# A gated-delta scan whose two heads share each TensorE operand: k and q side by side, u with zeros between

## The chip, the cores and the metric

The kernel runs on one core of one Trainium2 chip. The metric is device time in microseconds of one execution, lower is better. Before the change it is 1455.97 us, the median of three runs (1453.89 to 1456.44).

## The reference, cut to what matters

One inference step of two layers over 1024 prompt frames and 64 sample frames of width 1024. The even layer (gated convolution and banded attention) is not touched. The odd layer is a gated DeltaNet with 8 heads of 128 x 128 state, run in chunks of 64 frames:

```python
def gdn_chunk(S, q, k, v, g, beta):
    ...
    u = sol[..., :HD_C] - jnp.einsum('bhlk,bhkv->bhlv', sol[..., HD_C:], S)
    qk = jnp.einsum('blhd,bmhd->bhlm', q, k) * decay
    o = jnp.einsum('blhk,bhkv->blhv', q * jnp.exp(gc)[..., None], S) + jnp.einsum('bhlm,bhmv->blhv', qk, u)
    g_last = gc[:, -1]
    k_dec = k * jnp.exp(g_last[:, None, :] - gc)[..., None]
    S_new = jnp.exp(g_last)[..., None, None] * S + jnp.einsum('blhk,bhlv->bhkv', k_dec, u)
    return S_new, o
```

`sol` holds the solutions of a unit triangular system per chunk; it does not depend on `S`. What does depend on `S` is the recurrence over the chunks: `u` from `S`, `S_new` from `u`, and the output `o` from both.

## The kernel before, in words

Everything is float32. Heads are taken in four pairs `p`; a head of a pair is `q` (0 or 1). There are 17 chunks `c` of a pair (16 of the prompt, one of the sample, which starts from a given state), in three batches `b` of 6, 6 and 5 chunks.

Two kinds of TensorE work are woven together. One is the long projections (`project`, tile `pjt`): float32r matmuls with 384 or 320 columns, three for each of eight blocks (hi x hi, lo x hi, hi x lo), so three `pjt` rows in a listing are one step of it. The other is the delta work on small tiles. A generator class `Order` writes out TensorE's order by hand: each piece of work yields a time in nanoseconds after which its next step may stand, a running estimate (`order.now`, raised by `mm` and `tr`) plays the clock, and the projections fill what lies between. The order on TensorE is therefore fixed in the built program; the other engines' orders are set by a scheduler when it is built.

The delta work of one pair and batch is: `prepare` (transposes of k and q, their norms, `kd` = k by rows times a decay, `kt` = k by rows, the products k by k and q by k that become `An` and `KQD`), `substitute` and `join` (the triangular inverse, built up in 32-wide pieces: matmuls that are named `XT,Cb`, `M,X`, `XT,An`, `M,X`), `solve` (three groups of matmuls `cst,vt`, `BD,kt`, `vr,BD`, whose results replace k and v in place), `scan` (the recurrence) and `finish` (norm of the output and a transpose of `o`). While one batch is scanned, the next is solved and the one after is prepared, so these share the engines.

A scan step before, for both heads of the pair:
- `ks`: k and q of each head, 64 columns each, times that head's state. Four matmuls with a 128 x 64 stationary operand.
- DVE makes `u` (tile `us`, L1140) from the first half of `ks` and the solved v; ACT scales the second half into `qs` (L1142).
- `su`: `kd` of each head times `u` of that head. Two matmuls, with 64 rows and 128 columns of the array, into two PSUM buffers. DVE makes the new state from them (L1154).
- the inner output `o`: `KQD` times `u`, two matmuls of 64 x 64. They do not stand behind `su` but at the head of the next step, just ahead of the next `ks` (`outputs(*last)`). DVE adds `qs` (L1109), ACT squares the sum (L1113).

Halves 0 to 63 and 64 to 127 of a tile's partitions are the two heads. PSUM buffers of the delta work: tag `tr` has two, shared by the transposes, `An`/`KQD`, the inverse, `solve` and `o`; `su` has two; `ks` has one.

Of the kernel before, what the change touches and what calls it, by code (L numbers as in the profile page):

```python
# [107 lines left out]
class Net:  # L108
# [624 lines left out]
    def odd(self):  # L733
# [72 lines left out]
        def new_kq(p):  # L806
            KQ[p] = k1.tile([P, 2, NCH, 2, 64], F32, name="kq", tag="kq", bufs=2)
# [4 lines left out]
        def conv_dst(p, i):  # L812
            q = i % 2
            if i < 2:
                return 8 + 2 * p + q, KQ[p][:, 0, :, q, :]
            if i < 4:
                return 2 * p + q, KQ[p][:, 1, :, q, :]
            return 16 + 2 * p + q, V[p][:, :, q, :]
# [23 lines left out]
        def gates(ba):  # L842
            for n in ("beta", "egc", "dec", "gc"):
                G[n] = comp(n)
            beta, egc, dec, gc = (G[n] for n in ("beta", "egc", "dec", "gc"))
            buf = G["buf"] = k1.tile([P, NCH * P], F32, name="dbuf", tag="vt", bufs=2)
            x, ab, gg = (buf[:, 68 * i:68 * i + 68].rearrange("p (a c) -> p a c", c=NCH) for i in range(3))
# [22 lines left out]
            for j, c0 in enumerate((C_U, C_BD, C_H, C_H + 1)):  # L870
                w = cst[:, c0:c0 + P] if j < 2 else cst[:, c0:c0 + 1].broadcast_to([P, P])
                self.mm(ps[:, 68 * j:68 * j + 68], w, gf)
            gcf = gc.rearrange("p a c -> p (a c)")
# [5 lines left out]
            act.activation(egl.rearrange("p q a c -> p (q a c)"), ps[:, 136:272], AF.Exp)  # L879
            yield 1500  # L880
# [30 lines left out]
        def zeroed():  # L911
            for name, w in (("Cb", 32), ("BD", P)):
                Z[name] = self.kp.tile([P, NBM, w], F32, name=name)
                pool.memset(Z[name], 0.0)

        def prepare(p, b):
# [16 lines left out]
            ss = self.kp.tile([P, 2, NBM], F32, name="ss", tag="ss", bufs=2)[:, :, :nb]  # L933
            rr = self.kp.tile([P, 2, NBM], F32, name="rr", tag="rr", bufs=3)[:, :, :nb]
            tmp = self.kp.tile([P, 2, NBM], F32, name="rt", tag="rt", bufs=2)[:, :, :nb]
            junk = self.kp.tile([P, P], F32, name="junk", tag="junk", bufs=1)
            for i0 in range(0, nb, 4):
                m = min(4, nb - i0)
                for a in range(2):
                    ps = pst("tr").rearrange("p (c j) -> p c j", j=P)  # L940
                    for i in range(m):
                        c = c0 + i0 + i
                        self.tr(ps[:, i, :], kq[:, a, c].rearrange("p q t -> p (q t)"))
                    for i in range(m):
                        act.activation(junk, ps[:, i, :], AF.Square, accum_out=ss[:, a, i0 + i:i0 + i + 1])  # L945
                    if a == 0:
                        act.copy(out=kt[:, i0:i0 + m, :], in_=ps[:, :m, :])
                        dve.tensor_tensor(kd[:, i0:i0 + m, :], ps[:, :m, :],
                                          dec[:, p, c0 + i0:c0 + i0 + m].unsqueeze(2).broadcast_to([P, m, P]), ALU.mult)
                    yield 2160  # L950
            dve.tensor_scalar(ss, ss, EPS, None, ALU.add)
# [7 lines left out]
            for i0 in range(0, nb, 4):  # L959
                m = min(4, nb - i0)  # L960
                ps = pst("tr").rearrange("p (c j) -> p c j", j=P)
                for i in range(m):
                    for q in range(2):
                        self.mm(ps[64 * q:64 * q + 64, i, :], kq[:, 0, c0 + i0 + i, q, :], kq[:, :, c0 + i0 + i, q, :], share=1.6)
# [102 lines left out]
        def solve(p, b):  # L1067
# [3 lines left out]
            for i0 in range(0, nb, 4):  # L1071
                m = min(4, nb - i0)
                vt = V[p][:, c0 + i0:c0 + i0 + m].rearrange("p c q t -> p c (q t)")
                k = KQ[p][:, 0, c0 + i0:c0 + i0 + m].rearrange("p c q t -> p c (q t)")
# [8 lines left out]
                act.copy(out=k, in_=ps[:, :m, :])  # L1083
# [9 lines left out]
        def scan(p, b):  # L1093
# [3 lines left out]
            egc, egl = G["egc"], G["egl"]  # L1097
            vt = V[p].rearrange("p c q t -> p c (q t)")
            S = state.get(p)

            def outputs(i, o4, so, u, qs):

                o = pst("tr")[:, 0:P]
                for q in range(2):
                    h = slice(64 * q, 64 * q + 64)
                    self.mm(o[h], KQD[h, i, :], u[h], share=1.6, tile_position=(64 * q, 64 * q))
                a = i % 4
                if qs is not None:
                    dve.tensor_tensor(o4[:, a, :], o, qs, ALU.add)  # L1109
                else:  # L1110
                    dve.tensor_copy(o4[:, a, :], o)
                junk = self.kp.tile([P, P], F32, name="junk", tag="junk", bufs=1)
                act.activation(junk, o4[:, a, :], AF.Square, accum_out=so[:, 0, a:a + 1])  # L1113
                if a == 3 or i == nb - 1:
                    order.add(f"fin{p}.{b}.{i - a}", 3, finish(p, b, i - a, a + 1, o4, so), [])

            last = None
            for i in range(nb):
                if i % 4 == 0:
# [5 lines left out]
                c = c0 + i  # L1125
# [5 lines left out]
                qs = None  # L1131
                if last:
                    outputs(*last)
                if S is not None:
                    ks = pst("ks")
                    for a in range(2):
                        for q in range(2):
                            self.mm(ks[64 * q:64 * q + 64, P * a:P * a + P], kq[:, a, c, q, :], S[:, q, :], share=1.6)
                    u = self.kp.tile([P, P], F32, name="us", tag="us", bufs=2)
                    dve.tensor_tensor(u, ks[:, 0:P], vt[:, c, :], ALU.add)  # L1140
                    qs = self.kp.tile([P, P], F32, name="qs", tag="qs", bufs=2)
                    act.activation(qs, ks[:, P:2 * P], AF.Copy, scale=egc[:, p, c:c + 1])  # L1142
                    yield 850
                else:
                    u = vt[:, c, :]
                su = []
                for q in range(2):
                    h = slice(64 * q, 64 * q + 64)
                    su.append(pst("su")[:, 0:P])
                    self.mm(su[q], kd[h, i, :], u[h])  # L1150
                Sn = self.kp.tile([P, 2, P], F32, name="S", tag="S", bufs=3)
                for q in range(2):
                    if S is not None:
                        dve.scalar_tensor_tensor(Sn[:, q, :], S[:, q, :], egl[:, q, p, c:c + 1], su[q], ALU.mult, ALU.add)  # L1154
                    else:
                        dve.tensor_copy(Sn[:, q, :], su[q])
                S = Sn
                last = i, o4, so, u, qs
                yield 1110
            outputs(*last)  # L1160
# [4 lines left out]
        def finish(p, b, i0, m, o4, so):  # L1165
# [16 lines left out]
            for q in range(2):  # L1182
                act.activation(ch(mo[:, q, :64 * m]), ps[:, :m, 64 * q:64 * q + 64], AF.Copy, scale=par[:, P_ON:P_ON + 1])
# [150 lines left out]
```

## Time and profile before

| what | value |
|---|---|
| runs | 1456.44, 1455.97, 1453.89 us |
| profiled execution, its own time | 1450.93 us |
| its span | 1449.1 us |
| TensorE busy (PE) | 1372.1 us, 95% |
| weight loads (PEld) | 1233.9 us, 85% |
| VectorE (DVE), ScalarE (ACT), GpSimd (POOL) | 877.6, 678.0, 312.9 us |
| first `ks` and last `su` | 796.0 and 1288.7 us |

Engines are named PE (TensorE), PEld (its weight loads), DVE, ACT, POOL and SP. A row of the timeline gives start, length, engine, line, operation, output<-inputs, the part of the array and the shape, and a count; in brackets stands the idle time ahead of it and what ended it. Plain float32 matmuls leave two records each, float32r matmuls and transposes one. A matmul's length there overlaps its neighbours', so times on PE are read below as the distance from one start to the next. L119 is the helper that issues every matmul and L124 the one that issues every transpose; the names of the tiles tell which is which.

### The profile page before, as it was taken

The numbers are of one execution on the slowest core, as the hardware profiler recorded it, in microseconds if no ns is written. First come the engines' busy times: TensorE is split into PE (matmuls) and PEld (weight loads), VectorE is DVE, ScalarE is ACT, GpSimd is POOL, SyncE is SP. The second block draws the span as 40 slices with busy tenths as digits, with TensorE's granted clock in tenths as the row PEclk, the third lists the DMA queues.
The fourth block names the chain that finished last, engine by engine and source line by source line (L and its number), as shares of the span: only waits on it lengthen the run. The fifth ranks groups of instructions, "written<-read, shape, count | busy, mean of one in ns | idle before, by whom it ended". The sixth has DMA issues, their size and how long they took to land. (4 is left out here: it accounts for less than half of the span.)

```text
span 1449.1 us, 28440 instructions
## 1 busy us (share of the span) xinstructions
PE 1372.1 (95%) x10600; PEld 1233.9 (85%) x10600; DVE 877.6 (61%) x2497; ACT 678.0 (47%) x1776; POOL 312.9 (22%) x810
## 2 busy tenths in 40 slices
PE   8999999999999999899878999999899989998996
PEld 6989998998999899888768778788887877888985
DVE  7675257137435754777887768676765756433654
ACT  7643345144334456675546444544453534323642
POOL 3000000000100014420345325140523152210322
PEclk9999999999999999999989999999999999999998
DMA  7402111210210274541523112122211232337454
GB/s 260 143 16 89 57 52 52 80 53 26 90 61 30 66 244 135 190 140 37 119 73 79 40 29 77 33 52 44 68 30 31 62 95 67 95 123 234 141 197 162
DMA packets 114378, 133.12 MB, mean 92 GB/s; under 512 B 35568, under 2 KB 81336, under 8 KB 114240
## 3 DMA queue, kind: packets, MB, share of 16 engines
q1 hardware_dynamic: 83280, 105.01, 24.8%
q10 hardware_dynamic: 30960, 26.31, 5.6%
q8 instruction: 83, 1.36, 0.4%
q14 instruction: 55, 0.45, 0.1%
HBM read 99.91 MB, written 34.51 MB: 93 GB/s over the span
## 5 line engine op out<-in xcount | busy, mean ns | idle before, releaser
L119 PE MATMUL pjt<-hhi,wlo 128*128 128x384 f32 (+1 forms) x1768 | 617.7, 349 | 1.5 <-DVE wlo L165 1.5
L119 PE MATMUL pjt<-hhi,whi 128*128 128x384 f32 (+1 forms) x1768 | 583.7, 330 | 5.8 <-ACT whi L164 2.4
L119 PE MATMUL pjt<-hlo,whi 128*128 128x384 f32 (+1 forms) x1768 | 576.1, 330 | 0.7 <-DVE hlo L391 0.6
L119 PEld LDWEIGHTS pjt<-hhi,wlo 128*128 128x128 f32 x1768 | 337.6, 191 | 25.6 <-issue 11.7
L119 PEld LDWEIGHTS pjt<-hhi,whi 128*128 128x128 f32 x1768 | 337.6, 191 | 12.4 <-ACT whi L164 3.7
L119 PEld LDWEIGHTS pjt<-hlo,whi 128*128 128x128 f32 x1768 | 335.6, 190 | 1.8 <-DVE hlo L391 1.8
L165 DVE TENSOR_TENSOR wlo<-wf,whi 128x512 fp32r<-128x512 f32 x222 | 154.3, 721 | 153.0 <-ACT whi L164 149.5
L164 ACT CAST whi<-wf 128x512 fp32r<-128x512 f32 x222 | 129.6, 618 | 165.0 <-PE pjt L119 123.4
L612 ACT ACTIVATE pr<-pr,mx 128x640 f32<-128x640 f32 (+5 forms) x72 | 50.9, 707 | 89.4 <-DVE mx L611 88.9
L784 DVE SCALAR_TENSOR_TENSOR kq<-pjt,par,kq 128x384 f32<-128x384 f32 (+2 forms) x144 | 71.6, 497 | 2.9
L348 POOL TENSOR_TENSOR sqa<-sqa,sq 128x384 f32<-128x384 f32 (+1 forms) x36 | 39.7, 1103 | 151.7 <-ACT sq L346 151.6
L573 POOL MEMSET bias<- 64x64 f32 x8 | 1.3, 163 | 321.0 <-DMA bias<-Gd 228.2
L609 DVE CUSTOM_DVE_ANT_0 pr<-sc,bias 128x640 f32<-128x640 f32 (+5 forms) x72 | 48.0, 666 | 26.7 <-PE sc L119 25.9
L991 POOL TENSOR_TENSOR px<-AL 48x14 f32<-48x14 f32 (+6 forms) x168 | 46.9, 279 | 61.5 <-DMA AL<-Sd 52.5
L1154 DVE SCALAR_TENSOR_TENSOR S<-S,egl,su 128x128 f32<-128x128 f32 x128 | 40.6, 343 | 29.3 <-PE su L119 28.9
L755 POOL TENSOR_TENSOR so<-so 128x4 f32<-128x4 f32 (+2 forms) x72 | 16.7, 232 | 175.4 <-DVE so L748 117.2
L945 ACT ACTIVATE junk<-tr 128x128 f32<-128x128 f32 x136 | 37.7, 277 | 33.9 <-PE tr L124 29.6
L992 POOL TENSOR_TENSOR AL<-AL,px 48x14 f32<-48x14 f32 (+6 forms) x168 | 46.8, 278 | 9.4
L119 PE MATMUL pjt<-mhi,whi 128*128 128x384 f32 x128 | 44.4, 347 | 3.7 <-ACT mhi L164 3.7
L124 PE MATMUL pt<-cst,pr 128*128 128x128 f32 (+1 forms) x280 | 43.4, 270 | 4.5 <-DVE pr L614 2.9
L1113 ACT ACTIVATE junk<-o 128x128 f32<-128x128 f32 x68 | 21.0, 309 | 51.4 <-DVE o L1109 42.2
L119 PE MATMUL pjt<-mlo,whi 128*128 128x384 f32 x128 | 44.5, 348 | 0.3 <-DVE mlo L165 0.2
(250 smaller groups left out, 2210.8 us busy)
## 6 DMA issues: line engine op xcount, KB each, us to landing
wf<-in_w_in SPq DMA_DIRECT2D x128, 256.0 KB, 3.5
wf<-in_w_out SPq DMA_DIRECT2D x96, 256.0 KB, 3.5
mf<-mixd SPq DMA_DIRECT2D x32, 192.0 KB, 3.4
x<-in_x SPq DMA_DIRECT2D x8, 384.0 KB, 6.2
xg<-in_x SPq DMA_DIRECT2D x2, 1536.0 KB
xd<-xg SPq DMA_DIRECT2D x2, 1536.0 KB
Dd<-dbuf ACTq DMA_DIRECT2D x16, 192.0 KB, 2.1
od<-o ACTq DMA_DIRECT2D x12, 256.0 KB, 2.5
```

The lines of the kernel that those rows point to most:

```text
L119: return self.pe.matmul(out, lhsT=lhsT, rhs=rhs, start=start, stop=stop, **k)
L124: return self.pe.transpose(out, in_, self.ident[0:k, 0:k])
L164: self.act.copy(out=hi, in_=x)
L165: (eng or self.dve).tensor_tensor(lo, x, hi.bitcast(F32), ALU.subtract)
L348: pool.tensor_tensor(acc, acc, sq, ALU.add)
L609: dve.tensor_tensor_reduce(out=cut(pr[0:nq, :nk]), in0=sc[0:nq, :nk // nw, :nw], in1=cut(b["bias"][a][0:nq, j0:j0 + nk]), scale=1.0, scala ...
L612: act.activation(pr[0:nq, :nk], pr[0:nq, :nk], AF.Exp, bias=mx[0:nq, 1:2], scale=1.0, accum_out=mx[0:nq, 2:3])
L784: dve.scalar_tensor_tensor(oi, ch(ps[:, i0 + j + 1:i0 + j + 1 + m]), cw[j], oi, ALU.mult, ALU.add)
L945: act.activation(junk, ps[:, i, :], AF.Square, accum_out=ss[:, a, i0 + i:i0 + i + 1])
L991: pool.tensor_tensor(t, AL[:, j + 1:16, j:j + 1].broadcast_to([lanes, m, w]), x.broadcast_to([lanes, m, w]), ALU.mult)
L992: pool.tensor_tensor(o, o, t, ALU.add)
L1154: dve.scalar_tensor_tensor(Sn[:, q, :], S[:, q, :], egl[:, q, p, c:c + 1], su[q], ALU.mult, ALU.add)
```

## The change

A pair's k and q now lie in one tile as four blocks of 64 for each chunk: k of head 0, q of head 0, q of head 1, k of head 1. So `ks` is one 128 x 128 stationary operand for each head, two matmuls in place of four, and the two heads' results lie in two columns of `ks`. `u` of both heads is one tile of 128 x 256 with zeros in the two blocks that belong to no head; two such tiles are zeroed once. `su` is one matmul of `kd` with 256 columns. DVE makes `u` and ACT scales q's part in two operations of 64 partitions each where there was one of 128; ACT writes straight into the output tile `o4`. The inner output is written directly behind `su`, and its two 64 x 64 matmuls go to the other half of the partitions (head 0 in the upper). In `prepare` the transposes are of k and q together, `kt` is copied in two halves, and `kd` is made from `kt`. The number of transposes and of the other matmuls is the same. The yields of a step are 1050 and 1110 where they were 850 and 1110.

```diff
 def new_kq(p):
-    KQ[p] = k1.tile([P, 2, NCH, 2, 64], F32, name="kq", tag="kq", bufs=2)
+    KQ[p] = k1.tile([P, NCH, 4, 64], F32, name="kq", tag="kq", bufs=2)
...
 def zeroed():
-    for name, w in (("Cb", 32), ("BD", P)):
+    for name, sh in (("Cb", [P, NBM, 32]), ("BD", [P, NBM, P]), ("u0", [P, 2, P]), ("u1", [P, 2, P])):
...
 def prepare(p, b):
...
-    for a in range(2):
+    for q in range(2):
         ps = pst("tr").rearrange("p (c j) -> p c j", j=P)
         for i in range(m):
-            c = c0 + i0 + i
-            self.tr(ps[:, i, :], kq[:, a, c].rearrange("p q t -> p (q t)"))
+            self.tr(ps[:, i, :], kq[:, c0 + i0 + i, 2 * q:2 * q + 2, :].rearrange("p a t -> p (a t)"))
...
-        if a == 0:
-            act.copy(out=kt[:, i0:i0 + m, :], in_=ps[:, :m, :])
-            dve.tensor_tensor(kd[:, i0:i0 + m, :], ps[:, :m, :], ...
+        h = slice(64 * q, 64 * q + 64)
+        act.copy(out=kt[h, i0:i0 + m, :], in_=ps[h, :m, :])
         yield 2160
+    dve.tensor_tensor(kd[:, i0:i0 + m, :], kt[:, i0:i0 + m, :], ...
...
 def scan(p, b):
...
-    if last:
-        outputs(*last)
+    u = Z[f"u{c % 2}"]
     if S is not None:
         ks = pst("ks")
-        for a in range(2):
-            for q in range(2):
-                self.mm(ks[64 * q:64 * q + 64, P * a:P * a + P], kq[:, a, c, q, :], S[:, q, :], share=1.6)
-        u = self.kp.tile([P, P], F32, name="us", tag="us", bufs=2)
-        dve.tensor_tensor(u, ks[:, 0:P], vt[:, c, :], ALU.add)
-        qs = self.kp.tile([P, P], F32, name="qs", tag="qs", bufs=2)
-        act.activation(qs, ks[:, P:2 * P], AF.Copy, scale=egc[:, p, c:c + 1])
-        yield 850
+        for q in range(2):
+            self.mm(ks[:, col[q]], kq[:, c, 2 * q:2 * q + 2, :].rearrange("p a t -> p (a t)"), S[:, q, :])
+        for q in range(2):
+            dve.tensor_tensor(u[half[q], q, :], ks[half[q], col[q]], vt[half[q], c, :], ALU.add)
+        for q in range(2):
+            o = half[1 - q]
+            act.activation(o4[o, a, :], ks[o, col[q]], AF.Copy, scale=egs[o, p, c:c + 1])
+        yield 1050
...
-    for q in range(2):
-        h = slice(64 * q, 64 * q + 64)
-        su.append(pst("su")[:, 0:P])
-        self.mm(su[q], kd[h, i, :], u[h])
+    su = pst("su")[:, 0:2 * P]
+    self.mm(su, kd[:, i, :], u.rearrange("p q j -> p (q j)"))
...
+    o = pst("tr")[:, 0:P]
+    for q in range(2):
+        self.mm(o[half[1 - q]], KQD[half[q], i, :], u[half[q], q, :], share=1.6, tile_position=(64 * q, 64 - 64 * q))
+    if S is not None:
+        dve.tensor_tensor(o4[:, a, :], o, o4[:, a, :], ALU.add)
...
     yield 1110
-    outputs(*last)
```

In the orders below `tr<-us,KQD` (before) and `tr<-u_7069,KQD` (after) are the inner output, `tr<-cst,vt`, `tr<-BD,kt` and `tr<-vr,BD` the three groups of `solve`, `tr<-kq` the products that become `An` and `KQD`. TensorE, first pair, where the scan of batch 0 meets the solve of batch 1; before:

```order
L119 MATMUL tr<-M,X 32x32 x12
L119 MATMUL pjt<-hhi_6899,wlo 128x320
L119 MATMUL pjt<-hhi_6899,whi 128x320
L119 MATMUL pjt<-hlo_6900,whi 128x320
L119 MATMUL tr<-us,KQD 64x128 x2
L119 MATMUL ks<-S,kq 64x128 x4
L124 MATMUL tr<-cst,vt 128x128 x4
L119 MATMUL tr<-BD,kt 128x128 x4
L119 MATMUL su<-us,kd 128x128 x2
L119 MATMUL tr<-kq 64x128 x8
L119 MATMUL tr<-vr,BD 128x128 x4
L119 MATMUL tr<-us,KQD 64x128 x2
```

and now:

```order
L119 MATMUL ks<-S,kq 128x128 x2
L119 MATMUL tr<-M,X 32x32 x12
L119 MATMUL tr<-kq 64x128 x8
L119 MATMUL su<-u_7069,kd 128x256
L119 MATMUL tr<-u_7069,KQD 64x128 x2
L124 MATMUL tr<-cst,vt 128x128 x4
L119 MATMUL tr<-BD,kt 128x128 x4
L119 MATMUL ks<-S,kq 128x128 x2
L119 MATMUL tr<-kq 64x128 x2
```

The products `tr<-kq` have moved ahead of `su`, and the output stands between `su` and the first group of `solve`, where `ks` stood. The same engine a little earlier, where the inverse of batch 1 begins; before:

```order
L119 MATMUL tr<-us,KQD 64x128 x2
L119 MATMUL ks<-S,kq 64x128 x4
L119 MATMUL tr<-XT,Cb 32x16 x24
L124 MATMUL tr<-cst,kq 128x128
L119 MATMUL pjt<-hhi_6477,wlo 128x384
```

and now:

```order
L119 MATMUL su<-u_7069,kd 128x256
L119 MATMUL tr<-u_7069,KQD 64x128 x2
L124 MATMUL tr<-cst,kq 128x128
L119 MATMUL tr<-XT,Cb 32x16 x24
L119 MATMUL pjt<-hhi_6477,wlo 128x384
```

A transpose of `prepare` has moved from behind the inverse's first group to ahead of it. On DVE, the rows that follow the two `BD` copies out of `tr` at the first of the two places; before:

```order
L1063 TENSOR_TENSOR BD<-tr,sT 32x6x32 x2
L784 SCALAR_TENSOR_TENSOR kq<-pjt,par,kq 128x6x64
L752 TENSOR_TENSOR rt<-rt,rr 128x2x5
L1109 TENSOR_TENSOR o_8324<-tr,qs 128x128
L784 SCALAR_TENSOR_TENSOR kq<-pjt,par,kq 128x6x64
```

and now:

```order
L1071 TENSOR_TENSOR BD<-tr,sT 32x6x32 x2
L784 SCALAR_TENSOR_TENSOR kq<-pjt,par,kq 128x6x64
L751 SCALAR_TENSOR_TENSOR rt<-rr,ss 128x2x5
L1145 SCALAR_TENSOR_TENSOR S<-S,egl,su 128x128 x2
L784 SCALAR_TENSOR_TENSOR kq<-pjt,par,kq 128x6x64
L752 TENSOR_TENSOR rt<-rt,rr 128x2x5
L1153 TENSOR_TENSOR o_8339<-tr,o_8339 128x128
```

The addition that empties the output's PSUM buffer now stands behind the two state updates of the same step.

More of the change, by code (lines that the diff above doesn't have):

```diff
@@ L814, in conv_dst @@
             if i < 2:
[L815 removed]
+                return 8 + 2 * p + q, KQ[p][:, :, 3 * q, :]
             if i < 4:
[L817 removed]
+                return 2 * p + q, KQ[p][:, :, 1 + q, :]
             return 16 + 2 * p + q, V[p][:, :, q, :]
@@ L842, in gates @@
         def gates(ba):
-            for n in ("beta", "egc", "dec", "gc"):
+            for n in ("beta", "egc", "egs", "dec"):
                 G[n] = comp(n)
-            beta, egc, dec, gc = (G[n] for n in ("beta", "egc", "dec", "gc"))
+            beta, egc, dec = (G[n] for n in ("beta", "egc", "dec"))
             buf = G["buf"] = k1.tile([P, NCH * P], F32, name="dbuf", tag="vt", bufs=2)
+            gc = G["gc"] = buf[:, 1600:1668].rearrange("p (a c) -> p a c", c=NCH)
             x, ab, gg = (buf[:, 68 * i:68 * i + 68].rearrange("p (a c) -> p a c", c=NCH) for i in range(3))
@@ L872, in gates @@
                 self.mm(ps[:, 68 * j:68 * j + 68], w, gf)
+            for q in range(2):
+                self.mm(ps[64 * q:64 * q + 64, 272:340], cst[:, C_U + 64 - 64 * q:C_U + 128 - 64 * q], gf)
             gcf = gc.rearrange("p a c -> p (a c)")
@@ L1082, in solve @@
                     self.mm(ps[:, i, :], kt[:, i0 + i, :], BD[:, i0 + i, :])
-                act.copy(out=k, in_=ps[:, :m, :])
+                act.copy(out=k, in_=ps[:, :m, :].rearrange("p c (q t) -> p c q t", q=2))
                 yield 900
@@ L1096, in scan @@
             kd, KQD = rr["kd"], rr["KQD"]
-            egc, egl = G["egc"], G["egl"]
+            egs, egl = G["egs"], G["egl"]
             vt = V[p].rearrange("p c q t -> p c (q t)")
+            half = [slice(0, 64), slice(64, P)]
+            col = [slice(0, P), slice(P, 2 * P)]
             S = state.get(p)
-            def outputs(i, o4, so, u, qs):
-                o = pst("tr")[:, 0:P]
-                for q in range(2):
-                    h = slice(64 * q, 64 * q + 64)
[L1106 to L1117, printed above, removed]
             for i in range(nb):
-                if i % 4 == 0:
+                c, a = c0 + i, i % 4
+                if a == 0:
                     if len(fins) > 2:
@@ L1153, in scan @@
                     if S is not None:
-                        dve.scalar_tensor_tensor(Sn[:, q, :], S[:, q, :], egl[:, q, p, c:c + 1], su[q], ALU.mult, ALU.add)
+                        dve.scalar_tensor_tensor(Sn[:, q, :], S[:, q, :], egl[:, q, p, c:c + 1], su[:, col[q]], ALU.mult, ALU.add)
                     else:
-                        dve.tensor_copy(Sn[:, q, :], su[q])
+                        dve.tensor_copy(Sn[:, q, :], su[:, col[q]])
+                o = pst("tr")[:, 0:P]
+                for q in range(2):
+                    self.mm(o[half[1 - q]], KQD[half[q], i, :], u[half[q], q, :], share=1.6, tile_position=(64 * q, 64 - 64 * q))
+                if S is not None:
+                    dve.tensor_tensor(o4[:, a, :], o, o4[:, a, :], ALU.add)
+                else:
+                    dve.tensor_copy(o4[:, a, :], o)
                 S = Sn
-                last = i, o4, so, u, qs
+                junk = self.kp.tile([P, P], F32, name="junk", tag="junk", bufs=1)
+                act.activation(junk, o4[:, a, :], AF.Square, accum_out=so[:, 0, a:a + 1])
+                if a == 3 or i == nb - 1:
+                    order.add(f"fin{p}.{b}.{i - a}", 3, finish(p, b, i - a, a + 1, o4, so), [])
                 yield 1110
-            outputs(*last)
             if b == NB - 1:
```

31 lines of the change are left out of this document (16 added, 15 removed).

## The prediction

> **What bounds the kernel now.** I read the page first, then the busy time of the stretch in which the scans run, then TensorE's timeline inside a few scan steps, last the waits.
>
> ```profile
> span 1449.1 us, 28440 instructions
> ...
> PE 1372.1 (95%) x10600; PEld 1233.9 (85%) x10600; DVE 877.6 (61%) x2497; ACT 678.0 (47%) x1776; POOL 312.9 (22%) x810
> ```
>
> ```profile
> 796.00:1291.00 495.00, 473.69 (x4764) 394.00 (x4762) 321.30 (x1183) 219.97 (x751) 153.67 (x592) 0.99 0.24 59
> ```
>
> In the second row the columns are the stretch, its length, then busy time of PE, PEld, DVE, ACT and POOL, the granted clock, the DMA share and GB/s. All scan steps lie in it. PE idles for 495.0 - 473.7 = 21.3 us of it, the clock is full, DVE is busy for 65%, ACT for 44%. So the stretch ends when PE has worked off its list: PE time taken out of a step comes off the span, unless it turns into waiting. Since busy time on PE counts overlapping and draining matmuls, what a step really costs is read from the starts.
>
> ```profile
> 1226.45 0.34 PE L119 MATMUL pjt<-hlo,whi 128*128 128x384 f32 x1
> 1226.72 0.44 PE L119 MATMUL tr<-us,KQD 64*64 64x128 f32 x4
> 1227.09 0.66 PE L119 MATMUL ks<-S,kq 128*64 128x128 f32 x8
> 1227.68 0.44 PE L119 MATMUL pjt<-hhi,wlo 128*128 128x384 f32 x1
> 1227.96 0.34 PE L119 MATMUL pjt<-hhi,whi 128*128 128x384 f32 x1
> 1228.13 0.34 PE L119 MATMUL pjt<-hlo,whi 128*128 128x384 f32 x1
> ...
> 1228.65 0.34 PE L119 MATMUL pjt<-hlo,whi 128*128 128x384 f32 x1
> 1228.92 0.49 PE L119 MATMUL su<-us,kd 64*128 64x128 f32 x4
> 1229.35 0.44 PE L119 MATMUL pjt<-hhi,wlo 128*128 128x384 f32 x1
> 1229.63 0.34 PE L119 MATMUL pjt<-hhi,whi 128*128 128x384 f32 x1
> ```
>
> Projection matmuls of 384 columns start 0.17 to 0.18 us apart (0.175 below). From the last one ahead of the output (1226.45) to the second behind `ks` (1227.96) are 1.51 us; two steady distances of 0.175 taken off, output and `ks` cost 1.16 us. From 1228.65 to 1229.63, `su` costs 0.98 - 0.35 = 0.63 us. A step costs PE 1.79 us. Part of it is no streaming: the distance into the output and into `su` is 0.27 instead of 0.175, and the first projection matmul behind a group holds the next off by 0.28.
>
> **The change, part by part.** What the new shapes cost is read from full-array float32 matmuls with projections on both sides, and from an output group that follows such matmuls directly:
>
> ```profile
> 791.85 0.34 PE L119 MATMUL pjt<-hlo,whi 128*128 128x384 f32 x1
> 792.03 0.61 PE L119 MATMUL tr<-vr,BD 128*128 128x128 f32 x4
> 792.39 0.42 PE L119 MATMUL pjt<-hhi,wlo 128*128 128x384 f32 x1
> 792.65 0.34 PE L119 MATMUL pjt<-hhi,whi 128*128 128x384 f32 x1
> ...
> 818.35 0.31 PE L119 MATMUL pjt<-hlo,whi 128*128 128x320 f32 x1
> 818.49 0.61 PE L119 MATMUL tr<-vr,BD 128*128 128x128 f32 x4
> 819.03 0.44 PE L119 MATMUL tr<-us,KQD 64*64 64x128 f32 x4
> 819.39 0.41 PE L119 MATMUL pjt<-hhi,wlo 128*128 128x320 f32 x1
> 819.64 0.31 PE L119 MATMUL pjt<-hhi,whi 128*128 128x320 f32 x1
> ```
>
> `ks`: two float32 matmuls of 128 x 128 (four records) are exactly the first group: 792.65 - 791.85 - 0.35 = 0.45 us. There is no extra distance into it (0.18).
> `su` and output: the new `su` is one matmul of 256 columns, which streams as many columns as the four records of 128, so I take it at the price of `tr<-vr,BD`; the second group then is the new pair `su`, output: 819.64 - 818.35 - 2 x 0.15 = 0.99 us (0.15 is the steady distance at 320 columns). The other half of the partitions for the output changes nothing that these rows show; I cost it at nothing.
> New step: 0.45 + 0.99 = 1.44 us, 0.35 less. How many steps, and what the other engines do in them:
>
> ```profile
> L119 PE MATMUL ks<-S,kq 128*64 128x128 f32 x512 | 42.1, 285 | 0.0
> ...
> L1140 DVE TENSOR_TENSOR us<-ks,vt x64: 251/292/294, 796.7 to 1287.4; 128x128 f32<-128x128 f32 x64
> L1142 ACT ACTIVATE qs<-ks,egc x64: 349/368/405, 797.6 to 1287.7; 128x128 f32<-128x128 f32 x64
> ```
>
> 64 steps have a state (8 records each): 64 x 0.35 = 22 us less PE time. The four first chunks without a state change by less than half a microsecond together.
>
> ```profile
> L164 ACT CAST whi<-wf 128x512 fp32r<-128x512 f32 x222 | 129.6, 618 | 165.0 <-PE pjt L119 123.4
> ...
> L508 ACT CAST ks<-ks 64x512 fp32r<-64x512 f32 x8 | 5.0, 619 | 0.2
> L947 ACT COPY kt<-tr 128x512 f32<-128x512 f32 x12 | 7.0, 580 | 0.0
> ```
>
> The two casts of 512 elements take the same on 64 and on 128 partitions, so I price each half of a split operation like the whole. DVE: one more addition per step at 0.29 us: 64 x 0.29 = 19 us, and eight copies of u for the first chunks. 321 + 21 of 495 us: 69%, still beside PE. ACT: one more scaling of 0.37 in each step, 24 us, and the second copies of `kt`, twelve at 0.58 and twelve shorter ones, at most 14 us: 220 + 38 = 258 us, 52%. What hides both is the projection matmuls. In the order, nine now usually stand between `ks` and `su` (1.6 us) where six stood (1.05); that covers the second addition. Where that cover is missing, `su` waits 0.29 us longer. `kd` read from `kt` and not from PSUM, two zeroed tiles, two small matmuls and one exponential in `gates`: under 1 us on PE; I take 1 us for the longer `prepare` at the first pair, where nothing is scanned yet.
>
> **What comes back as waiting.** The output takes one of the two `tr` buffers. It used to stand where `ks` (0.59 us) came behind it; now the next `tr` user is often directly behind. The built program says which buffer each gets. At the first place shown in the orders, `M,X`, the output, `cst,vt` and `BD,kt` all have the same one, one after the other: `cst,vt` can start only when DVE has done both state updates and the output's addition, `BD,kt` only when ACT has copied `vr`. This is so in all four pairs. At the second place `cst,kq` and `XT,Cb` share one in two pairs (in a third, output and `XT,Cb` with a single transpose between). With two more, there are 13 places at which a `tr` user stands at once behind its predecessor in the same buffer. Before there are five, plus four with one short group between. Their price, from the rows of before:
>
> ```profile
> 814.62 0.43 PE L119 MATMUL tr<-us,KQD 64*64 64x128 f32 x4 [0.68 <-ACT vt L1088]
> ...
> 816.48 0.68 PE L119 MATMUL tr<-BD,kt 128*128 128x128 f32 x4 [0.24 <-DVE KQD L967]
> 852.48 0.66 PE L124 MATMUL tr<-cst,o 128*128 128x128 f32 x4 [1.38 <-ACT M L1050]
> 862.50 0.49 PE L119 MATMUL tr<-BD,kt 128*128 128x128 f32 x2 [0.66 <-ACT vr L1079]
> 927.31 0.33 PE L124 MATMUL tr<-cst,kq 128*128 128x128 f32 x1 [0.79 <-ACT M L1050]
> ...
> 1082.33 0.44 PE L119 MATMUL tr<-us,KQD 64*64 64x128 f32 x4 [0.68 <-ACT vt L1088]
> ```
>
> Five waits of 0.66 to 1.38, mean 0.84, sum 4.2, and four of 0.24: 5 us, which go. 13 x 0.84 = 11 come, and about 1 for the outputs that wait for `M,X`: 12. Ends: nothing comes, if DVE and ACT happen to be ahead (-5 us net); 13 x 1.38 = 18, and nothing goes (+18). I take +7, from the mean, as the new places are of the same kind.
>
> **Sum.** -22 + 7 + 1, and +1 for `su` where its cover is short: -13 us. The profiled execution took 1450.9 us (span 1449.1 and 1.8 around it), 5.0 below the median of the runs, so 1438 for such an execution and 1443 for the median. Ends: -22 - 5 = -27 gives 1429, -22 + 18 + 2 = -2 gives 1454. Behind the last output 34 projection matmuls stand ahead of the last transpose of `finish`, 40 before: at most 1 us less cover, inside these ends.
>
> [...]
>
> **Rivals.**
> Full gain: the new `tr` places cost no more than the old ones. DVE idles for 31% of the stretch even then, and PE comes to these places no later than now. -20 to -27, about 1433. Against it: the four links in one buffer are a chain by construction.
> Gain eaten: the waits return 19 to 25 us, within 0.2% of before (3 us, about what a measurement of this kernel can tell from no change); 1456. For it: in the crowded places `An` and `KQD` come out of a chain on DVE, so PE arriving earlier only waits longer, and 22 us are no more than 5.6 per pair. Against: the crowded places hold five or six of a pair's 16 steps; the others have nine projection matmuls on each side.
> Slower, by one mechanism: DVE's addition of the output stands behind the two state updates and needs what ACT has written into `o4`. If ACT is late, DVE stands still, the next `u` is late, and `su` waits in every step. It decides from 0.35 us a step on; at 0.5 us, 64 x 0.5 - 22 = +10, about 1466. For it:
>
> ```profile
> PE su L119 <- DVE us L1140: 3.3, 2, 2.6
> ```
>
> Such waits exist, two of 64 now, 3.3 us. Against: ACT has from `ks` to the end of `su`, over 2 us, for two operations of 0.37.
> [...]
>
> **How the numbers follow.** Forecast (-4 to -19): 0.50; full gain 0.26; eaten 0.10; overlap lost 0.03; slower 0.11. Faster by over 0.2%: 0.76; within: 0.13; slower: 0.11. The range leaves out the slower case and the far end of the full gain: 1430 to 1457. The forecast's own range is 1437 to 1452.
>
> **What the profile of the changed kernel would show.** Right: `ks` in four records, 0.36 us from its start to the next projection, no 0.27 ahead of it; `su` in two records, 0.43 to 0.54 to the output; per pair some 3 us of waits of PE at `cst,vt` (ended by DVE's addition of the output) and `BD,kt` (by ACT's `vr`); the last `su` near 1275 instead of 1288.7. Wrong: `su` or the moved output longer than taken here; PE waiting for `u` in many steps; idle time in the stretch above 40 us.

## The result and the profile after

The changed kernel takes 1477.62 us, median of four runs (1475.43 to 1481.26), against 1456.2 beside it: ratio 1.0166, 95% interval 1.0135 to 1.0197. (The ratios here and in the table below come from the record; they are not exactly the quotients of the medians, which here would give 1.0147.) It is slower by 21 us where 13 us less were forecast. Its profiled execution took 1479.56 us, span 1477.8; the page of it:

```profile
span 1477.8 us, 27890 instructions
...
PE 1369.1 (93%) x10212; PEld 1251.3 (85%) x10212; DVE 897.8 (61%) x2581; ACT 714.4 (48%) x1865; POOL 310.1 (21%) x812
```

The same stretch as before (columns: stretch, length, busy time of PE, PEld, DVE, ACT, POOL, granted clock, DMA share, GB/s):

```profile
796.00:1291.00 495.00, 449.00 (x4253) 392.84 (x4252) 333.33 (x1237) 247.71 (x817) 150.14 (x584) 0.96 0.23 54
```

PE now idles for 46 us of it (21.3 before), and the clock has fallen from 0.99 to 0.96. The last `su` starts at 1316.0, not at 1288.7.

A step itself costs what was forecast, where it is read here. PE's timeline, first `su` and output, then `ks`:

```profile
1222.90 0.34 PE L119 MATMUL pjt<-hlo,whi 128*128 128x384 f32 x1
1223.08 0.59 PE L119 MATMUL su<-u,kd 128*128 128x256 f32 x2
1223.60 0.43 PE L119 MATMUL tr<-u,KQD 64*64 64x128 f32 x4
1223.96 0.44 PE L119 MATMUL pjt<-hhi,wlo 128*128 128x384 f32 x1
1224.24 0.34 PE L119 MATMUL pjt<-hhi,whi 128*128 128x384 f32 x1
...
1225.12 0.60 PE L124 MATMUL tr<-cst,kq 128*128 128x128 f32 x4
1225.55 0.61 PE L119 MATMUL ks<-S,kq 128*128 128x128 f32 x4
1225.92 0.42 PE L119 MATMUL pjt<-hhi,wlo 128*128 128x384 f32 x1
```

From 1222.90 to 1224.24 are 1.34 us; two steady distances of 0.175 off, `su` and output cost 0.99, as forecast. `ks` takes 0.37 to the next start.

What PE waits for between 780 and 1340 us (total, times, longest), after:

```profile
PE tr L124 <- DVE o L1176: 18.7, 5, 7.1
PE tr L124 <- DVE o L1153: 6.0, 5, 1.5
PE tr L119 <- ACT kt L953: 4.7, 7, 1.5
PE pjt L119 <- DVE pjt L778: 3.9, 2, 2.9
PE su L119 <- DVE u L1131: 2.9, 2, 1.8
PE tr L119 <- ACT vr L1087: 2.7, 4, 0.7
```

and the row of before that answers to the first of these (L1175 there is the same line):

```profile
PE tr L124 <- DVE o L1175: 4.4, 2, 3.1
```

The second and the last rows of after are the forecast chain in one `tr` buffer. The first is not: it is `finish`, whose transposes of `o` wait for DVE's scaling by the norm. And `su <- u`, the mechanism of the slower rival, is 2.9 us, less than the 3.3 of before.

**The long wait followed back.** Of the 18.7 us the longest three are 5.07 us (at 877.34), 4.13 (1031.77) and 7.14 (1194.76). The first of them, from after's timelines of PE, DVE, POOL and ACT:

```profile
871.89 0.38 PE L119 MATMUL tr<-vr,BD 128*128 128x128 f32 x2
877.34 0.66 PE L124 MATMUL tr<-cst,o 128*128 128x128 f32 x2 [5.07 <-DVE o L1176]
```

```profile
858.78 0.28 DVE L1153 TENSOR_TENSOR o<-tr,o 128x128 f32<-128x128 f32 x1
871.07 0.16 DVE L1170 SCALAR_TENSOR_TENSOR so<-so,rr 128x2 f32<-128x2 f32 x1
876.71 0.16 DVE L1174 SCALAR_TENSOR_TENSOR so<-so,rr 128x2 f32<-128x2 f32 x1 [3.33 <-POOL so L758]
876.90 0.48 DVE L1176 TENSOR_SCALAR o<-o,so 128x128 f32<-128x128 f32 x2
```

```profile
872.12 0.19 POOL L755 TENSOR_TENSOR so<-so 128x2 f32<-128x2 f32 x1 [16.64 <-DVE so L748]
873.67 1.47 POOL L964 TENSOR_TENSOR kt<-kt,kap 128x768 f32<-128x768 f32 x1
876.48 0.20 POOL L758 TENSOR_TENSOR so<-so 128x2 f32<-128x2 f32 x1
```

```profile
861.91 0.28 ACT L951 ACTIVATE junk<-tr 128x128 f32<-128x128 f32 x1 [2.50 <-PE tr L124]
870.47 0.27 ACT L1087 COPY vr<-tr 128x128 f32<-128x128 f32 x1
870.63 0.32 ACT L1158 ACTIVATE junk<-o 128x128 f32<-128x128 f32 x1
```

The last output of the group is complete at 859.06. Its square comes 11.6 us later: in ACT's order it stands behind `prepare`'s squares and copies (L951, L953) and behind `vr`, and these need transposes that PE does only later, so ACT stood idle for 2.5 us with the square's input ready. Then come 4.6 us on POOL (872.12 to 876.68) with the product on `kt` in between, then DVE. Going through all 24 groups this way, the square ends 11.9, 5.6 and 4.6 us behind the addition in just the three with the long waits, at most 2.0 in the others. Before, the longest is 2.6.

**The clock.** Half clock lies in blocks of 3.4 us behind such waits. Stretches of after around the wait at 877, and around one of 1.52 us at `cst,vt`:

```profile
877.30:882.70 5.40, 5.36 (x33) 4.29 (x33) 1.98 (x9) 1.88 (x5) 0.00 (x0) 0.50 0.08 24
882.70:888.00 5.30, 5.30 (x38) 4.27 (x34) 4.81 (x17) 2.13 (x12) 0.00 (x0) 1.00 0.24 74
```

```profile
814.40:817.80 3.40, 1.84 (x17) 1.05 (x14) 3.22 (x14) 1.36 (x5) 0.00 (x0) 1.00 0.01 2
817.80:824.60 6.80, 6.12 (x28) 5.20 (x27) 4.36 (x25) 2.08 (x6) 3.67 (x13) 0.50 0.11 28
```

In PE's timeline projection matmuls of 320 columns start 0.27 us apart in such a block and 0.14 behind it:

```profile
881.17 0.47 PE L119 MATMUL pjt<-hhi,whi 128*128 128x320 f32 x1
881.44 0.47 PE L119 MATMUL pjt<-hlo,whi 128*128 128x320 f32 x1
...
883.08 0.31 PE L119 MATMUL pjt<-hhi,whi 128*128 128x320 f32 x1
883.22 0.31 PE L119 MATMUL pjt<-hlo,whi 128*128 128x320 f32 x1
```

**Where the 28.7 us of span went.** I split each profiled span in three: *idle*, the gaps between the end of one matmul and the next start; *lost*, half of the time in which PE is busy in blocks of clock 0.5; and the rest, *work*, which is PE's work at full clock with 1 us ahead of the first matmul and some 13 us behind the last. The first two are added up over PE's whole timeline.

| kernel | span | idle | lost | work |
|---|---|---|---|---|
| before | 1449.1 | 63.1 | 22.3 | 1363.7 |
| after | 1477.8 | 94.7 | 37.0 | 1346.0 |
| difference | +28.7 | +31.6 | +14.7 | -17.7 |

The gain in work is there. Waiting eats it nearly twice over, and the lower clock behind the waits takes half as much again. The two profiled executions stand further apart than the medians (28.7 against 21.4 us), since that of before (1450.93 us) is quicker than the runs its median is taken of.

### The profile page after: what moved, and what is told of

It is laid out like the page before. It is cut to its first block, busy times and chain, and to the rows that moved or that the text cites. A ratio compares the mean times of both kernels' runs of the same rounds, so it can differ in the third digit from the quotient of the medians.

```text
span 1477.8 us, 27890 instructions
## 1 busy us (share of the span) xinstructions
PE 1369.1 (93%) x10212; PEld 1251.3 (85%) x10212; DVE 897.8 (61%) x2581; ACT 714.4 (48%) x1865; POOL 310.1 (21%) x812
## 5 line engine op out<-in xcount | busy, mean ns | idle before, releaser
L119 PE MATMUL pjt<-hhi,whi 128*128 128x384 f32 (+1 forms) x1768 | 585.6, 331 | 11.8 <-DVE pjt L778 3.9
L119 PEld LDWEIGHTS pjt<-hhi,wlo 128*128 128x128 f32 x1768 | 339.5, 192 | 20.6 <-issue 11.6
L612 ACT ACTIVATE pr<-pr,mx 128x640 f32<-128x640 f32 (+5 forms) x72 | 50.9, 707 | 89.4 <-DVE mx L611 88.8
L1134 ACT ACTIVATE o<-ks,egs 64x128 f32<-64x128 f32 x128 | 46.4, 363 | 48.9 <-DVE u L1131 36.7
L609 DVE CUSTOM_DVE_ANT_0 pr<-sc,bias 128x640 f32<-128x640 f32 (+5 forms) x72 | 48.0, 666 | 26.7 <-PE sc L119 25.9
L999 POOL TENSOR_TENSOR px<-AL 48x14 f32<-48x14 f32 (+6 forms) x168 | 47.3, 282 | 75.2 <-DMA AL<-Sd 65.8
L1131 DVE TENSOR_TENSOR u<-ks,vt 64x128 f32<-64x128 f32 x128 | 36.7, 287 | 29.4 <-PE ks L119 28.1
L951 ACT ACTIVATE junk<-tr 128x128 f32<-128x128 f32 x136 | 37.5, 276 | 23.2 <-PE tr L124 17.0
L1145 DVE SCALAR_TENSOR_TENSOR S<-S,egl,su 128x128 f32<-128x128 f32 x128 | 39.0, 343 | 15.5 <-PE su L119 14.6
```

What stands on the lines that cost most here:

```text
L119: return self.pe.matmul(out, lhsT=lhsT, rhs=rhs, start=start, stop=stop, **k)
L609: dve.tensor_tensor_reduce(out=cut(pr[0:nq, :nk]), in0=sc[0:nq, :nk // nw, :nw], in1=cut(b["bias"][a][0:nq, j0:j0 + nk]), scale=1.0, scala ...
L612: act.activation(pr[0:nq, :nk], pr[0:nq, :nk], AF.Exp, bias=mx[0:nq, 1:2], scale=1.0, accum_out=mx[0:nq, 2:3])
L951: act.activation(junk, ps[:, i, :], AF.Square, accum_out=sx[:, q, i0 + i:i0 + i + 1])
L999: pool.tensor_tensor(t, AL[:, j + 1:16, j:j + 1].broadcast_to([lanes, m, w]), x.broadcast_to([lanes, m, w]), ALU.mult)
L1134: act.activation(o4[o, a, :], ks[o, col[q]], AF.Copy, scale=egs[o, p, c:c + 1])
```

## The experiments

All were timed beside the kernel before, in five groups with a median of it for each (1452.0 to 1454.8); the difference to this median is given. Idle, lost and work are of the profiled execution, as above. It can lie off the median: those of fin14 and late_tr3 are the longest of their runs (7.5 and 10.7 us over), those of y1050_old and y850 lie 7.6 and 4.7 us under.

| kernel | median us | difference | ratio, 95% interval | idle | lost | work |
|---|---|---|---|---|---|---|
| fin14 | 1468.34 | +13.5 | 1.0104 (1.0067 to 1.0140) | 89.4 | 35.6 | 1349.0 |
| tr3 | 1460.26 | +5.4 | 1.0036 (1.0017 to 1.0055) | 83.5 | 28.4 | 1345.5 |
| out_late | 1466.65 | +11.8 | 1.0088 (1.0068 to 1.0108) | 86.3 | 28.9 | 1350.7 |
| out_early_old | 1478.64 | +23.8 | 1.0166 (1.0140 to 1.0192) | 85.8 | 31.2 | 1362.5 |
| late_tr3 | 1461.85 | +7.9 | 1.0062 (1.0032 to 1.0092) | 90.1 | 33.3 | 1347.4 |
| tr3_fin14 | 1453.11 | -0.8 | 0.9984 (0.9962 to 1.0006) | 80.4 | 28.6 | 1346.1 |
| y1050_old | 1466.99 | +13.1 | 1.0091 (1.0067 to 1.0116) | 73.5 | 20.9 | 1363.3 |
| y850 | 1470.72 | +16.8 | 1.0107 (1.0073 to 1.0140) | 89.7 | 22.9 | 1351.6 |
| noscale | 1454.60 | +2.6 | 1.0006 (0.9976 to 1.0036) | 80.1 | 25.0 | 1348.2 |
| noscale_old | 1453.79 | +1.8 | 1.0003 (0.9980 to 1.0026) | 63.9 | 22.5 | 1364.4 |
| newton_dve | 1470.97 | +19.0 | 1.0119 (1.0079 to 1.0159) | 96.3 | 26.1 | 1348.2 |
| tr3_fin24_newton | 1447.48 | -4.5 | 0.9966 (0.9945 to 0.9987) | 75.2 | 26.6 | 1346.7 |
| out_early_old_noscale | 1460.70 | +6.3 | 1.0045 (1.0023 to 1.0067) | 71.8 | 26.8 | 1361.8 |
| tr3_noscale | 1445.55 | -8.8 | 0.9949 (0.9932 to 0.9967) | 77.4 | 20.7 | 1346.1 |
| best_join | 1450.47 | -3.9 | 0.9973 (0.9952 to 0.9994) | 73.9 | 28.9 | 1346.0 |
| sq_dve | 1464.88 | +11.0 | 1.0079 (1.0050 to 1.0108) | 89.0 | 26.7 | 1347.8 |
| tr3_sq_dve | 1448.49 | -5.4 | 0.9964 (0.9947 to 0.9981) | 75.2 | 25.8 | 1347.2 |
| tr3_fin14_sq_dve | 1445.97 | -7.9 | 0.9947 (0.9931 to 0.9964) | 75.6 | 27.2 | 1345.7 |

One thing holds in all rows: work is 1362 to 1364 with the old shapes and 1346 to 1352 with the joined ones. Most of what else differs lies in the two columns ahead of it.

**Each suspect alone.** A later `finish`, a third `tr` buffer (taken from `su`), the output back at the head of the next step; and, in the kernel before, the output directly behind `su` and nothing else.

```diff
 # fin14: finish
-    yield 9000
+    yield 14000
 # tr3: pst
-    bufs=2 if tag in ("tr", "su") else 1)
+    bufs=3 if tag == "tr" else 1)
 # out_late: scan, at the step's head and once behind the loop (the inner output's lines gone behind su)
+    if last:
+        outputs(*last)
...
+    outputs(*last)
 # out_early_old: scan of the kernel before
-    if last:
-        outputs(*last)
...
-    last = i, o4, so, u, qs
+    outputs(i, o4, so, u, qs)
...
-    outputs(*last)
```

> The changed kernel, with one number altered: finish places its transposes 14000 ns of the planner's clock behind the norm, where it says 9000. Theory finish: TensorE stands at these transposes because the norm's chain (ACT's square, DVE, GpSimd, DVE's scaling L1176) comes later than their fixed place; the five waits on L1176 (18.7 us, the longest 7.1) go, and with them most of the 27 us at half clock around them; 1450 to 1458 us. Theory tr buffers: those waits are a small part, the output's place behind su is what costs; 1470 to 1478 us. Theory prepare: no change, 1477 us.

> The changed kernel with three PSUM buffers of tag tr in place of two, and one of su in place of two (su is one matmul now, and the next one waits for the state anyway). Theory tr buffers: the waits at cst,vt for the output's addition (6.0 us) and at BD,kt and XT,Cb for ACT's copies (some 8 us) go, and 10 us at half clock; 1457 to 1464 us. Theory finish: the scaling is as late as before, 1472 to 1478 us. If the one su buffer costs, ks or su waits for DVE's state update in many steps and it gets slower than 1480.

> The changed kernel with the one part undone: the inner output stands again at the head of the next step, ahead of ks, and finish follows it; the joined ks and su stay. Theory tr buffers: the chain output, cst,vt, BD,kt in one buffer is broken, about 14 us of waits and 5 us of clock are saved, and the switch from the output's 64 x 64 tiles to ks costs as much as the one behind su did; 1455 to 1462 us. Theory finish: the chain behind the norm is as long as it was and its transposes are counted from the output as before, so 1472 to 1480 us. Theory that the joined shapes themselves cost: 1477 or more.

> The kernel before with the one part done: its inner output directly behind su, everything else as it was (four ks, two su, qs added by DVE). Theory tr buffers: the place alone brings 10 to 20 us of waits and clock and some 6 us for an output that stands between projections by itself; 1470 to 1485 us. Theory that the joined shapes or prepare cost: no more than 1462 us.

tr3 gave back 16 of the 21 us, out_late 10, fin14 8. The old kernel lost 24 us by the output's place alone, with all its old shapes, so the place is enough to cost as much as the whole change does. In tr3's trace the waits of `cst,vt` for the output's addition are gone (6.0 us in the changed kernel), and those on the copies of `kt` are 0.7 us in place of 4.7. The waits on the scaling stay in all four (16.5 us in out_late); the rows of fin14, tr3 and out_early_old:

```profile
PE tr L124 <- DVE o L1176: 10.6, 3, 8.0
```

```profile
PE tr L124 <- DVE o L1176: 18.2, 6, 6.0
```

```profile
PE tr L124 <- DVE o L1172: 15.1, 5, 9.3
```

fin14 leaves a wait of 8.0 us, so 5 us more distance doesn't reach: in this run ACT ends the square of three groups 9.7 to 10.5 us behind the addition.

**Together, and the spacing alone.** late_tr3 and tr3_fin14 join two of these edits each. y1050_old gives the kernel before the changed kernel's wider planned distance between `ks` and `su`, y850 gives the changed one the old distance.

```diff
 # y1050_old, in before; y850 the other way, in after
-    yield 850
+    yield 1050
```

> The changed kernel with the output back at the head of the next step and three tr buffers (one of su): both remedies at once, which alone gave 1466.7 and 1460.3 us. If both remove the same chain in the tr buffers, they do not add: 1457 to 1463 us. If the place costs something of its own besides the buffers (finish counted from an output that stands earlier, a DVE order that mixes it with the state updates), they add: 1443 to 1452 us.

> The changed kernel with three tr buffers and finish's transposes 14000 ns behind the norm. Theory finish: with three buffers 18 us of waits for DVE's scaling (L1176) are left, and 27 us at half clock beside them; they go to a third, 1442 to 1452 us. If only the buffers matter: 1457 to 1463 us, as with 9000.

> The kernel before with one number altered: 1050 ns of the planner's clock between ks and su where it says 850, so that TensorE's order gets the spacing of the changed kernel without its shapes or its output place. Theory that any new order costs, because waits fall at new places: 1462 to 1475 us. Theory that the place of the output and the tr buffers are the cause: 1451 to 1460 us.

> The changed kernel with 850 between ks and su as before. If the wider spacing is what costs (scans that end later): 1460 to 1470 us. If not: 1472 to 1485 us, and somewhat more waits of su for u, since DVE's second addition has 0.5 us less cover.

The late output gains nothing once `tr` has three buffers. tr3_fin14 is back at the time of before. And 0.2 us more planned distance costs the old kernel 13 us; its profiled execution was at the low end of its runs (1457.86 to 1473.67), and even there the waits on the scaling are 14.2 us, against 4.4 before:

```profile
PE tr L124 <- DVE o L1175: 14.2, 3, 7.6
```

So in the order of before `finish` was just early enough: two edits of the old kernel, this one and out_early_old, bring 10 us more of these waits. That they are what costs y1050_old its 13 us is not shown; it has no version without the scaling.

The old spacing gives the changed kernel 5 of its 21 us back, and y850's profile shows why no more. Its waits on the scaling fall from 18.7 to 5.0 us, but all others between 780 and 1340 us rise from 30.1 to 37.1, `su <- u` among them, which is 2.9 in the changed kernel:

```profile
PE tr L119 <- DVE KQD L975: 10.9, 5, 5.6
PE su L119 <- DVE u L1131: 7.7, 8, 4.8
...
PE tr L124 <- DVE o L1176: 5.0, 3, 2.4
```

A wait taken away at one place of this order can come back at another.

**`finish` taken away.** noscale and noscale_old leave out the scaling in the changed kernel and in the one before, so the transposes of `o` wait for the output's addition only. newton_dve keeps it and computes its reciprocal square root on DVE. tr3_fin24_newton adds three `tr` buffers to that and plans the transposes 24 us, not 9, behind the scaling.

```diff
 # noscale, noscale_old: finish
-    for i in range(m):
-        dve.tensor_scalar(o4[:, i, :], o4[:, i, :], fa[:, i:i + 1], None, ALU.mult)
 # newton_dve: finish
-    rsqrt(fa, va, tm, pool)
+    rsqrt(fa, va, tm, dve)
```

> The changed kernel without the scaling of the outputs by their norm (the DVE multiplications ahead of finish's transposes; that part of the computation is left out), so that the transposes of o wait for nothing but the addition of the output. Theory (finish's late chain): the 18.7 us of waits on the scaling go and with them most of the half-clock stretches behind them (27 us long, 13 us lost): 1450 to 1460. Rival (any respacing of the hand order costs, and a wait taken away at one place comes back at the next): 1466 or more, with the sum of the other waits larger by over 10 us.

> Control: the kernel before, without the same scaling. In its trace the transposes of o wait 4.4 us for it, two times. Theory (finish's chain is late only where the output stands directly behind the state's product): 1449 to 1455, so at most 5 us are gained, against 18 or more in the changed kernel. Rival (the scaling costs as much in both): 10 us or more gained here too.

> The changed kernel with the norm's reciprocal square root on DVE (9 short instructions) and not on POOL (12, in between those of the substitution and the 1.46 us product on kt). At 877 us POOL took 4.6 us of the chain from the last output to the scaling, and ACT's late square 12 us. Theory (chain through ACT and POOL): the waits on the scaling shrink from 18.7 to 5 to 10 us, the time to 1462 to 1470. Rival (POOL isn't what makes it late, or DVE, which now stands behind ACT's square with 9 instructions, holds up u and S): no change, 1475 or more.

> The changed kernel with 3 buffers for tr (su 1), the norm's reciprocal square root on DVE and finish's transposes planned 24 us behind its scaling, not 9. With 3 buffers and 14 us the time was 1453.1 and 15.5 us of waits on the scaling were left. Theory (these waits are what is left of the loss): they go, 1437 to 1447, below the kernel before. Rival (the order of the other waits was fitted to the old step, and they grow when finish moves): 1450 to 1460.

The scaling is worth 19 us in the changed kernel (+21.4 to +2.6) and nothing that can be measured in the one before, where the same 68 operations are taken off DVE. Idle falls by 14.6 and the clock's loss by 12.1 us: one cause, two prices of about the same size. Part of the waiting comes back: between 780 and 1340 us the 18.7 us on the scaling are gone, and all other waits rise from 30.1 to 40.2. The longest rows of noscale, of which the third has no counterpart in the changed kernel (before has 3.7 us there):

```profile
PE tr L124 <- DVE o L1153: 6.0, 5, 1.5
PE pjt L119 <- DVE pjt L778: 5.1, 2, 4.1
PE pjt L119 <- ACT mhi L164: 4.1, 1, 4.1
```

So the rival in noscale's expectation had its waits, 10 us more elsewhere, and not its time.

newton_dve gained only 2 us of 21 and missed the 1462 to 1470 by 1 us. Its waits on the scaling did shrink from 18.7 us, but not to the 5 to 10 expected:

```profile
PE tr L124 <- DVE o L1176: 13.2, 5, 4.0
```

tr3_fin24_newton is under the kernel before, with the scaling in, though it missed its 1437 to 1447 by half a microsecond.

**Two causes, or one?** out_early_old_noscale takes the scaling from the old shapes with the early output; tr3_noscale takes both suspects from the changed kernel; best_join is tr3_fin24_newton with more planned time for the load of `Xf`, behind which PE waited 8.3 us for `XT`.

```diff
 # best_join: join
-    yield 2790
+    yield 5500
```

> The kernel before with only the place of the output changed (directly behind the state's product), and without the scaling of the outputs by their norm (left out of the computation). With the scaling this place alone cost 24 us. Theory (the early output costs by finish's late chain: 12.5 us of waits on the scaling and the half clock behind them): 1453 to 1462. Rival (the order around the step is fitted, and any other place of the output costs by waits elsewhere, as 200 ns more spacing did with 13 us): 1466 or more.

> The changed kernel with 3 buffers for tr (su 1) and without the scaling (left out of the computation): both causes taken away at once. tr3 alone took 1460.3 with 18.2 us of waits on the scaling left, the scaling's leaving alone 1454.6 with about 14 us of waits at the tr places left. Theory (two separate causes that add): 1434 to 1444, which is what the prediction gave. Rival (waits move to the next producer that is late): 1450 or more.

> The kernel with 3 tr buffers, the norm's square root on DVE and finish 24 us later (1447.5), with the first products of join planned 5.5 us behind the load of Xf, not 2.79. Its longest waits left were 7.55, 3.15 and 5.15 us on XT, behind the load of Xf, each with a half-clock stretch after it. Theory (a plan that follows the real latency takes them away and the clock with them): 1430 to 1442. Rival (the next late producer takes their place): 1446 to 1455.

Without the scaling the early output costs the old shapes 6 us, not 24: three quarters of its price is `finish`. In the changed kernel tr3 alone takes off 16, the scaling alone 19, both 30: nearly a sum. It lands 8.8 us under before, 1.6 over the upper end that I had set. That this lies within the prediction's own 4 to 19 us is partly luck: the third buffer is no part of the predicted kernel. best_join is the failure of the series. The waits on `XT` shrank from 8.3 to 6.1 us, those of `su` on `u` grew from 2.1 to 9.3, and the time against before stayed (-3.9 and -4.5 us):

```profile
PE su L119 <- DVE u L1131: 9.3, 7, 5.0
PE tr L119 <- DVE XT L1029: 6.1, 2, 3.9
```

**Which engine makes `finish` late.** DVE squares the output directly behind its addition, in place of ACT, and writes the squares over the `v` that is used up.

```diff
 # sq_dve: scan
-    act.activation(junk, o4[:, a, :], AF.Square, accum_out=so[:, 0, a:a + 1])
+    dve.tensor_tensor_reduce(out=vt[:, c, :], in0=o4[:, a, :], in1=o4[:, a, :], scale=1.0, scalar=0.0,
+                             op0=ALU.mult, op1=ALU.add, accum_out=so[:, 0, a:a + 1])
```

> The changed kernel with the square of each output on DVE (directly behind the addition, written over the v that is used up) and not on ACT; nothing else. In the changed kernel ACT took the square 11.9, 5.6 and 4.6 us after the addition in 3 of 24 groups (0.3 to 2 us in the others), and the 3 waits on the scaling of over 4 us are these three. Theory (ACT's order makes finish late): the three waits shrink below 1 us or to what POOL alone makes of them, the sum on the scaling from 18.7 to under 6, the time to 1455 to 1465. Rival (POOL's square root in between the substitution makes it late, or 20 us more on DVE hold up u): 1470 or more.

> The same with 3 buffers for tr (su 1); finish at 9 us as it was. tr3 alone took 1460.3 with 18.2 us of waits on the scaling. Theory: as without the scaling (1445.6), plus what DVE's 68 squares delay: 1443 to 1452. Rival (DVE becomes late for u and S): 1455 or more.

> 3 buffers for tr, finish 14 us later, the square on DVE. tr3 with finish 14 us took 1453.1 with 15.5 us of waits on the scaling left. Theory (they go with the square): 1440 to 1448, under the kernel before. Rival (other waits grow, as with the finish 24 us later): 1448 to 1455.

In sq_dve two of the three long waits on the scaling are gone (those at 877 and 1032 us; at the second place PE still waits 2.9 us, now for `KQD`). The third stays at 5.3 us. There the square is in time and POOL's square root is late: from 1176.0 to 1182.0 us its twelve steps alternate with those of the substitution, and another product on `kt` stands in between. The rows of sq_dve and of tr3_fin14_sq_dve:

```profile
PE tr L124 <- DVE o L1176: 9.3, 4, 5.3
PE pjt L119 <- DVE vt L784: 6.5, 1, 6.5
```

```profile
PE tr L119 <- DVE XT L1029: 8.5, 2, 5.8
PE tr L119 <- ACT vr L1087: 6.4, 4, 3.2
```

The sum on the scaling is halved, not under 6 as expected, and a new wait of 6.5 us has come up in a projection. By these single profiles ACT's order makes about half of the waits on the scaling (18.7 to 9.3), POOL's square root some 30% (to 13.2 in newton_dve); the time is at the upper end of the expectation. With three `tr` buffers the square on DVE comes to 1448.49, as expected. With `finish` planned 14 us behind its scaling as well, 0.8 us of waits on the scaling are left: 1445.97 us, ratio 0.9947 (0.9931 to 0.9964). This version computes everything and beats both kernels. What the old shapes would gain from three `tr` buffers or from the square on DVE is open: no run gives these to the kernel before, so its lead is not shown to be the joined shapes' alone.

## Why the prediction was wrong, point by point

- *What bounds the kernel* ("the stretch ends when PE has worked off its list"): right as far as it went. Work on PE fell, and what came in its place was PE's waiting and its clock. "The clock is full" was read as a fact about the stretch; the clock was granted at 0.99 where PE idled for 21.3 us of it, and at 0.96 where PE idled for 46.
- *Step price, 64 x 0.35 = 22 us less, and 1 more in `prepare`*: right in kind and nearly in size. Work fell by 17.7 us over the whole kernel, where 21 were taken. The 0.99 us of `su` and output are met to the hundredth at the step shown.
- *DVE and ACT beside PE*: right for their load. The halves cost what was taken (medians, after):

```profile
L1131 DVE TENSOR_TENSOR u<-ks,vt x128: 269/289/296, 802.9 to 1314.8; 64x128 f32<-64x128 f32 x128
L1134 ACT ACTIVATE o<-ks,egs x128: 347/363/365, 804.7 to 1315.5; 64x128 f32<-64x128 f32 x128
```

- *"What comes back as waiting", +7 us*: this is the step that failed, as a term of the sum. The places that it names are there, and about as long as it says. One of the four in a chain:

```profile
817.46 0.79 PE L124 MATMUL tr<-cst,vt 128*128 128x128 f32 x4 [1.52 <-DVE o L1153]
818.93 1.44 PE L119 MATMUL tr<-BD,kt 128*128 128x128 f32 x5 [0.68 <-ACT vr L1087]
```

  The rows at such places (6.0, 4.7 and 2.7 above) add up to 13.4 us; 12 were taken. What was left out is twice that. First, `finish`, +14.3 us (18.7 of waits on the scaling against 4.4): the text has it only at the very end ("at most 1 us less cover"). It asked which buffer a moved output takes, and not what starts from it. 24 times a norm starts from it, through ACT, DVE, POOL and DVE again, at a planned distance of 9 us, and the square goes into ACT's order at another place. Without the scaling 19 of the 21 us are gone, with three buffers 16, without both 30. Second, the clock: +14.7 us, priced at nothing. All in all the term of +7 stands against 31.6 us more idle time and 14.7 of clock.
- *The first pair, +1 us*: too small in this execution, and the cause is open. The first `su` starts 6.1 us later (799.75 against 793.61), with 4.0 us more idle time and 1.7 more lost ahead of it. Between 680 and 780 us PE waits 3.8 us for ACT's copies of `kt`, and not at all in before; but no run took these alone away, and in the other versions of the changed kernel the first `su` starts anywhere from 793.5 (y850) to 805.3 (best_join).
- *Rivals*: "slower" came, by another mechanism than the one that stood for it; `su <- u` did not grow in it (2.9 against 3.3), though it is 7.5 to 9.3 in late_tr3, y850 and best_join. ACT does not start from `ks` on, as the text has it: its scaling waits for DVE's `u` (36.7 us over 34 times, 22.8 before), which delays PE's weight loads by 1.8 us in all. "Overlap lost" (0.03, at 1457; it supposes that the two halves of the old `su` ran at once on PE) did not come: the work fell by 17.7 us, and no row read here shows them so. In before the four records of `su` on 64 rows take 0.43 us to the next start (1228.92 to 1229.35), the four of `tr<-vr,BD` on all 128 rows 0.36 (792.03 to 792.39). "Eaten" had the right sense, PE arriving earlier only waits longer, but at 19 to 25 us it was too small, with neither `finish` nor the clock in it.
- *"Wrong: idle time in the stretch above 40 us"*: it is 46.

The range ended at 1457 and left the slower side out. The bound of +18 us for the waits came from five waits at `tr` places; the 3.1 us wait on the scaling stood in the profile of before and was not asked what it would do.

## What to carry to other kernels

When a product is moved in an order written by hand, list everything that starts from its result on the other engines, and look in the trace how long before its use each of them is ready now. An instruction added to ACT's order is priced by what stands ahead of it there and what that waits for, not by its length: the square at 870.63 is 0.32 us long and came 11.6 us late. And price a wait of PE with the clock it costs behind it; leaving out the scaling saved 14.6 us of idling and 12.1 of clock. Last, a wait that is taken out of such an order can come back at the next place, as in y850 and best_join: run the edit before counting its gain.

## What the hardware showed that I had not expected

The clock went down behind windows in which PE was half busy. The half-clock blocks lie on a fixed grid of 3.4 us: in both traces every change of the granted clock (25 in before, 35 in after) stands a whole multiple of 3.41 us from the first one. In after's window 814.40 to 817.80 above, PE is busy for 1.84 us, 54%, and the next two windows run at half speed. Sorting after's windows between 690 and 1300 us by PE's busy share: of those at full clock, every one below 0.47 was followed by a half-clock window, none above 0.57; between them it goes either way (PE's ends are modelled). In the same stretch of before and after together, each of the 13 full-clock windows under 0.40 was followed by half clock, and none of the 306 above 0.57. Busy time is not the whole measure: after's window 677.9 to 681.3 is 82% busy, most of it one group of 68 matmuls with 8 columns, and the next one ran at half speed.

So a single wait of 1.5 us could be enough where it lay whole in one window (1.52 us in the one at 814.4, 1.49 in the one at 855.4), though 1.79 us in the one at 1084.1 were not. The 1.38 us ahead of 852.48 in the kernel before were followed by no half-clock window: a border of the grid at 851.43 cuts them, and the window behind it is 69% busy.
